# Four accumulators for the last feed-forward's gate-up tiles, one modulation row set moved between feed-forwards, and two later context loads

## The chip, the core and the metric

The program runs on one NeuronCore of a Trainium2 chip. The metric is the device time of one execution in microseconds (us). Engines are named as in the profile: PE (TensorE), DVE (VectorE), ACT (ScalarE), POOL (GpSimd), SP (SyncE, which here issues nearly all loads).

## What is computed

The input `x` (256 tokens, 1024 wide) goes through a first block of two hybrid layers and then through a second block of two layers, whose core is:

```python
for l in range(DEPTH):                       # DEPTH = 2
    mod_l = jax.nn.silu(c) @ ada_w[l] + ada_b[l]        # nine rows: shift, scale, gate, three times
    mod_c = jax.nn.silu(c_ctx) @ ada_w[l] + ada_b[l]
    sh1, sc1, g1, sh2, sc2, g2, sh3, sc3, g3 = ...split(mod_l, 9)
    csh1, ..., cg3 = ...split(mod_c, 9)
    xl = post_norm(xl, 0.5 * g1 * swiglu(modulate(xl, sh1, sc1), ffn1_w_in[l], ffn1_w_out[l]))
    xc = post_norm(xc, 0.5 * cg1 * swiglu(modulate(xc, csh1, csc1), ffn1_w_in[l], ffn1_w_out[l]))
    yc, yl = even_mixer(...) if l % 2 == 0 else odd_mixer(...)
    xl = post_norm(xl, g2 * yl)
    xl = post_norm(xl, 0.5 * g3 * swiglu(modulate(xl, sh3, sc3), ffn2_w_in[l], ffn2_w_out[l]))
    if not last:
        xc = ...the same with the context's rows
```

`swiglu(h)` is `(silu(gate) * up) @ w_out` with `gate, up = split(h @ w_in, 2)`, 1024 to 2 x 2816 and back. `xc` starts as the context `ctx` (256 x 1024).

## The kernel before, in words

Every weight matrix product is done in three passes, high times high, low times high, high times low (L445, L446, L447). A weight tile of 128 x 1024 is loaded by SP into a buffer `wr`, ACT makes the high part `wh` (L353) and DVE the low part `wl` (L440). Rows to be multiplied are transposed on PE (L538) into PSUM, modulated (L569 on DVE, or ACT), and split into `XTH` (ACT) and `XTL` (DVE, L571).

In order of time: first block layer 0 and layer 1 (`layer1`, 0 to 343 us), the first feed-forward of second-block layer 0 ("f1", to 695), the even mixer (to 977) with its output projection, the second feed-forward "f2" of layer 0 (to 1351), "f1" of layer 1 (to 1735), the odd mixer (to 1931) and the last feed-forward, "f2" of layer 1 for the latent rows alone. `ffn_two` runs the three feed-forwards with 512 columns (X and C together), `ffn_one` the last one with 256.

**Modulation rows.** Each pair `(l, c)` is one of the nine rows of layer l; c = 2, 5, 8 are gates. Those in `V1`, `V2`, `V3` are made by the generator `ada_v` inside the three `ffn_two` calls: for each, eight steps, each a 512 KB load (`in_adav`) and two DVE multiply-and-sum instructions into `vj` (L675, one for each of the two conditions). A gate then takes a bias (L681), a transpose on PE into a bank F (L683), a copy on ACT into `vr` and a write to memory by POOL (`g<-vr`, L686). `gate_rows` reads it back, spread over all partitions, as `gb` on SP's queue; the output passes multiply by `gb` in L590 and L808 before adding to the rows (L592, L594, L812). `fillv` lets the generator go a share of a step per gate-up tile and per output step: `VR` holds these shares for the three calls, and `VS` is the number of the gate-up tile in the first group from which it may begin. What is left is issued at the start of the last output passes by `fillv(1000)`.

**First block.** `layer1(0)` projects the rows in three parts, `rows_of(0)`, `rows_of(1)`, `rows_of(2)` (L445 to L447 into pA). Other modulation rows are made there by PE itself (`ada`: L635, a stationary `cs` times the weight tile, into pG), with weight tiles from a ring of two buffers (`RING[0]`). Between them stand the scores of the first block's index selection (L1136 on PE, ACT `rl`, L1144 and L1146 on DVE, closed by the mask in L1149), and the row transposes L1099. The context rows `C` are loaded by two SP loads behind `rows_of(0)` (L1104, `dma_late`: issued after the last load before it in the program). Their first user is the context's transposes in layer 0 of the first block.

**PSUM.** The last feed-forward has a pool of its own, `ps4`: four banks A for the output passes, two banks B, of which each holds gate and up of one tile of 256 columns, and two banks F for the transposes (`self.trt` names the tag that `tr_rows` takes).

The order of instructions on each engine is set by the scheduler of the framework from the program's order, the waits and the buffers, so a change of buffers or of a loop's share moves instructions around it too.

Of the kernel before, what the change touches and what calls it, by code (L numbers as in the profile page):

```python
# [20 lines left out]
P = 128  # L21
# [185 lines left out]
OB = "B"  # L207
HN = (1, 2)
TK = ((3, 2), (1, 4))
VS = 5  # L210
VI = (1, 1, 1)
F2 = (3, 3)
PUTV = (0, 1)
# [8 lines left out]
PS1 = {"A": 2, "B": 3, "F": 2, "G": 1}  # L222
BT = dict(tr="B", ada="G", trp="B", pc="B", dd="B", kc="B", idx="B", sc="B", sc2="B", cmp="B", pt="B", pcm="B", pool="B", wt="F", out="FA")

V1 = ((0, 3), (0, 4), (0, 5), (0, 6), (0, 7), (0, 8))
V2 = ((1, 0), (1, 1), (1, 2), (1, 3))
V3 = ((1, 4), (1, 5), (1, 6), (1, 7), (1, 8))
VR = ((2.4, 0.5), (1.75, 0.25), (2.2, 0.25))
FF1 = (0.5, 0.4)
FF2 = (0.7, 0.7)  # L230
EVF = 0.05
# [12 lines left out]
class Kern:  # L244
# [95 lines left out]
    def need(self, l, c):  # L340

        while (l, c) not in self.done:
            if (l, c) in V1 + V2 + V3:
                self.fillv(1)
# [580 lines left out]
    def ffn_two(self, name, l, pool, order, after, fills=(0, 0), vr=(0, 0), early={}):  # L925
# [8 lines left out]
        for f0 in range(0, NFT, G):  # L934
# [17 lines left out]
            for ft in range(f0 if f0 else F0, f1):  # L952
                self.ffn_in(wi, ft, hid[ft - f0], slice(0, 512), slice(0, 512), pool, "B")
                self.fill(fills[0])
                if f0 or ft >= VS:
                    self.fillv(vr[0])
# [83 lines left out]
    def layer1(self, l, b1):  # L1040
        nc, A, X = self.nc, self.A, self.X
# [30 lines left out]
        def rows_of(j):  # L1072
            n, R = XS1_N[j], (R0, R1, R2)[j]
            outs = self.xs(src, offs[j], n, 0, 2)
            for m in range(2):
                if j == 2:

                    for kv in range(2):
                        self.act(dds[kv][:, m].rearrange("p (r w) -> p r w", w=64),
                                 outs[m][:, None, 64 * kv:64 * kv + 64].to_broadcast([P, 2, 64]))  # L1080
                    self.act(R[:, m, 128:], outs[m][:, 128:n])
                else:
                    self.act(R[:, m, :], outs[m][:, :n])
# [15 lines left out]
                    nc.tensor.transpose(pt[:, jj * 256 + m * P:jj * 256 + (m + 1) * P], sr[m], self.ident)  # L1099
            return pt[:, :256], pt[:, 256:]  # L1100
        rows_of(0)
        if l == 0:
            for m in range(2):
                self.dma_late(self.C[m], A["ctx"][m * P:(m + 1) * P, :])  # L1104
        self.rope(R0[:, :, 0:288].rearrange("p m (h w) -> p m h w", w=32), r8c, r8s, 4, "rp")
        wi = self.small([P, 2, 8], "wi")
        nc.vector.tensor_scalar_mul(wi, R0[:, :, 480:488], 1.0 / 16.0)
# [43 lines left out]
        def topk(place):  # L1151
            if TK[l][0] <= place < TK[l][0] + TK[l][1]:
                i = place - TK[l][0]
                n = 8 // TK[l][1]
                for r in range(n):
                    for m in MO:
                        mx8 = self.small([P, 8], "mx8")
                        nc.vector.max(mx8, works[m])
                        nc.vector.match_replace(works[m], mx8, works[m], -3.3e38)
                if i == TK[l][1] - 1:  # L1160
                    for m in MO:
                        nc.vector.tensor_scalar(works[m], works[m], -3.2e38, NEG, op0=OP.is_gt, op1=OP.mult)
# [12 lines left out]
                self.stack_q(QS[:, 2 * (j + jj)], QS[:, 2 * (j + jj) + 1], pp[jj])  # L1175
        topk(1)
        rows_of(2)
        topk(2)

        pe = self.cols[:, C_PE + 16 * l:C_PE + 16 * l + 16]  # L1180
        pc = self.bank(BT["pc"])
        for kv in range(2):
# [6 lines left out]
            for par in range(2):  # L1189
                ps = slice(64 * par, 64 * par + 64)  # L1190
# [723 lines left out]
    def run(self):  # L1914
        tc, nc, A = self.tc, self.nc, self.A
# [3 lines left out]
        with tc.tile_pool(name="xc", bufs=1) as xc:  # L1919
# [6 lines left out]
            with tc.tile_pool(name="b1", bufs=1) as b1:  # L1926
                self.tp = b1
                with tc.tile_pool(name="ps1", bufs=2, space=PSUM) as ps:
                    self.ps, self.banks, self.trt, self.adat = ps, PS1, BT["tr"], BT["ada"]
                    self.gens, self.ring = [self.ada(0, (0, 1)), self.ctx_first(0, NC)] + [  # L1930
                        self.ada(l, [c for c in range(9) if (l, c) not in V1 + V2 + V3 + ((0, 0), (0, 1))]) for l in range(2)], (b1, "wa", RING[0])
                    self.layer1(0, b1)
# [14 lines left out]
            with tc.tile_pool(name="ff1", bufs=1) as ff:  # L1947
                self.accp = ff
                self.ring = (ff, "wa", RING[1])
                self.vgen, self.vlate = self.ada_v(V1, ff), VI[0]  # L1950
                self.ffn_two("f1", 0, ff, (1, 0), lambda w: self.xt_mod(0, 3, w) if stage > 4 else None, FF1, VR[0], dict(enumerate(self.hc)))
                self.settle()
# [9 lines left out]
        with tc.tile_pool(name="xd", bufs=1) as xc:  # L1962
            self.rows(xc)
            for i, t in enumerate(self.X + self.C):
                nc.gpsimd.dma_start(t, save[i])
            with tc.tile_pool(name="mo", bufs=1) as g:
                self.gbn, self.accp = 2, g
                self.mixer_out(A["evo"], 0, g, lambda i: self.defer(lambda: self.xt_mod(0, 6, 0), DF[3]) if i
                               else self.xt_mod(0, 6, 1))
            if stage == 5:  # L1970
                return self.store()
            self.gbn, self.phase = 2, 1
            with tc.tile_pool(name="ff2", bufs=1) as ff:
                self.accp, self.ring = ff, (ff, "wa", RING[2])
                self.vgen, self.vlate = self.ada_v(V2, ff), VI[1]
                self.ffn_two("f2", 0, ff, (1, 0), lambda w: self.xt_mod(1, 0, w) if stage > 6 else None, FF2, VR[1])
                if stage == 6:
                    return self.store()
                self.vgen, self.vlate = self.ada_v(V3, ff, self.cb), VI[2]
                self.ffn_two("f1", 1, ff, (1, 0), lambda w: self.xt_mod(1, 3, w) if stage > 7 else None, (0, 0), VR[2])  # L1980
            if stage == 7:
                return self.store()
            with tc.tile_pool(name="nm", bufs=1) as e:
                self.NH = self.tl(e, [P, KD, 256], "NH", dt=F32R)
                self.NL = self.tl(e, [P, KD, 256], "NL", dt=F32R)
                self.gbn, self.accp, self.phase = 1, e, 3
                with tc.tile_pool(name="na", bufs=1) as e2:
                    V = self.odd_values(e2, (1, 0))
                    ps2.__exit__(None, None, None)
                    ps3 = tc.tile_pool(name="ps3", bufs=2, space=PSUM)  # L1990
                    self.ps, self.banks = ps3.__enter__(), {"P": 2, "S": 3, "T": 2, "O": 1}
                    self.ptn = 5
                    self.odd(e2, V)
                gb = self.ogb
                outs = self.xs(A["nao"], 0, 512, 0, 2, xh=self.NH, xl=self.NL, tag="P")
                for m in range(2):
                    self.accum(self.X[m], 0, outs[m], gb, True)
                if TL[8]:
                    self.xs_tail(A["nao"], 4096, 0, self.X, gb, self.NH, self.NL, "S")
                else:  # L2000
                    outs = self.xs(A["nao"], 4096, 512, 0, 2, xh=self.NH, xl=self.NL, tag="P", rows=ROWS)
                    for m in range(2):
                        self.accum(self.X[m], 1, outs[m], gb, True)
                    self.layernorm(self.X)
                ps3.__exit__(None, None, None)
            if stage == 8:
                return self.store()
            with tc.tile_pool(name="ps4", bufs=2, space=PSUM) as ps:
                self.ps, self.banks = ps, {"A": 4, "B": 2, "F": 2}
                with tc.tile_pool(name="ff3", bufs=1) as ff:  # L2010
                    self.accp, self.phase = ff, 4
                    self.xt_mod(1, 6, 0)
                    self.holdl = [self.lastn] * 4
                    for _ in self.ffn_one("f2", 1, 0, ff, 8):
                        pass
# [65 lines left out]
```

## Time and profile before

| | us |
|---|---|
| median of 3 runs (lowest to highest) | 2138.78 (2134.31 to 2139.55) |
| the profiled execution's own time | 2137.89 |
| its span in the trace | 2136.1 |
| PE busy | 2080.0 (97% of the span) |
| DVE busy | 1544.2 (72%) |
| ACT busy | 840.3 (39%) |

The profiled execution lies 0.89 us under the median. The 1.8 us between its time and its span lie outside what the trace shows. PE is the engine with the work: it is idle for 56 us in all. So the places to look at are those where PE is idle or where its granted clock is at the lower of its two levels (2.4 and 1.2 GHz; 1.00 and 0.50 of full speed in the rows); a mean clock of 0.74 over 20 us is 10.4 us at the lower level. Elsewhere DVE, ACT and SP cost nothing unless PE waits for them.

### The profile page before, as it was taken

Reading aid. Unit: us, or ns where it says so; the run is one execution under the profiler, and the core shown is the slowest. Engines: PE = TensorE matmul, PEld = TensorE weight load, DVE = VectorE, ACT = ScalarE, POOL = GpSimd, SP = SyncE. Lnnn points to the kernel's source line nnn. Section 1 sums busy time; section 2 is a strip of 40 time slices with the busy share of each in tenths; the row PEclk is TensorE's granted clock in tenths of the full one; section 3 lists DMA queues with packets and bytes.
Section 4 is the critical chain, followed back from the end, with each engine's and each line's share of the span. In section 5 each row is a group of like instructions: output and inputs, shape, how many; then the busy total and the mean of one; then the engine's idle time right before and its main releaser. Section 6 shows DMA issues by size and latency. Waiting matters only on the chain.

```text
span 2136.1 us, 30784 instructions
## 1 busy us (share of the span) xinstructions
PE 2080.0 (97%) x11967; PEld 1761.8 (82%) x11967; DVE 1544.2 (72%) x2839; ACT 840.3 (39%) x1460; POOL 19.6 (1%) x43
## 2 busy tenths in 40 slices
PE   7999999999999999899999999999999999998998
PEld 5898888988888788788888888888888888888997
DVE  6877866668879785958467757857786876776666
ACT  5555544322221544545312222531322245654443
POOL 0000000000000000000000000000000000000000
PEclk9999999999999999999999999999999999998999
DMA  8546444746654311133645543355555435425663
GB/s 273 183 150 189 143 146 148 241 154 209 194 169 142 121 54 43 30 107 123 203 150 158 157 151 116 109 172 183 162 174 160 145 119 155 112 80 152 187 185 119
DMA packets 92627, 318.77 MB, mean 149 GB/s; under 512 B 10652, under 2 KB 15868, under 8 KB 92480
## 3 DMA queue, kind: packets, MB, share of 16 engines
q1 hardware_dynamic: 88736, 307.44, 46.9%
q0 software_dynamic: 2400, 5.72, 0.8%
q10 hardware_dynamic: 1344, 3.64, 0.5%
q8 instruction: 94, 1.54, 0.3%
q14 instruction: 53, 0.43, 0.1%
HBM read 313.93 MB, written 3.20 MB: 148 GB/s over the span
## 4 chain that ended last, share of the span: by engine, by line
PE 88%; DVE 7%; ACT 2%; issue 2%; DMA 1%; ACTq 0%; DVEq 0%; SPq 0%
PE pB L445 13%; PE pB L446 13%; PE pB L447 13%; PE pA L446 10%; PE pA L445 10%; PE pA L447 10%; PE pF L445 2%; PE pF L446 2%; PE pF L447 2%; PE pB L1551 1%; PE pP L445 1%; PE pP L446 1%; DVE wl L440 1%; PE pP L447 1%; PE pO L1909 1%
## 5 line engine op out<-in xcount | busy, mean ns | idle before, releaser
L353 ACT ACTIVATE wh<-wr 128x1024 fp32r<-128x1024 f32 (+4 forms) x424 | 442.5, 1046 | 980.0 <-issue 456.1
L440 DVE TENSOR_TENSOR wl<-wr,wh 128x1024 fp32r<-128x1024 f32 (+4 forms) x424 | 509.7, 1204 | 293.9 <-ACT wh L353 289.6
L445 PE MATMUL pB<-XTH,wh 128*128 128x512 f32 (+1 forms) x1552 | 537.4, 347 | 6.8 <-DVE hid L452 2.9
L446 PE MATMUL pB<-XTL,wh 128*128 128x512 f32 (+1 forms) x1552 | 536.2, 346 | 0.3
L447 PE MATMUL pB<-XTH,wl 128*128 128x512 f32 (+1 forms) x1552 | 535.1, 345 | 0.0
L445 PEld LDWEIGHTS pB<-XTH,wh 128*128 128x128 f32 x1552 | 294.0, 190 | 47.7 <-ACT XTH L353 3.8
L446 PEld LDWEIGHTS pB<-XTL,wh 128*128 128x128 f32 x1552 | 294.4, 190 | 38.7 <-DVE XTL L571 0.9
L447 PEld LDWEIGHTS pB<-XTH,wl 128*128 128x128 f32 x1552 | 294.6, 190 | 37.7
L675 DVE SCALAR_TENSOR_TENSOR vj<-wr,cb 128x1024 f32<-128x1024 f32 x240 | 293.1, 1221 | 4.0
L447 PE MATMUL pA<-wh,hid 128*128 128x512 f32 (+1 forms) x624 | 239.5, 384 | 0.0
L446 PE MATMUL pA<-wl,hid 128*128 128x512 f32 (+1 forms) x624 | 239.2, 383 | 0.0
L445 PE MATMUL pA<-wh,hid 128*128 128x512 f32 (+1 forms) x624 | 238.1, 382 | 0.0
L446 PEld LDWEIGHTS pA<-wl,hid 128*128 128x128 f32 x624 | 117.2, 188 | 24.3
L445 PEld LDWEIGHTS pA<-wh,hid 128*128 128x128 f32 x624 | 117.2, 188 | 23.6
L447 PEld LDWEIGHTS pA<-wh,hid 128*128 128x128 f32 x624 | 117.2, 188 | 23.2
L445 PE MATMUL pA<-wh,XTH 128*128 128x512 f32 (+4 forms) x336 | 126.1, 378 | 3.6 <-ACT wh L353 1.8
L446 PE MATMUL pA<-wl,XTH 128*128 128x512 f32 (+4 forms) x336 | 125.1, 373 | 1.6 <-DVE wl L440 1.4
L447 PE MATMUL pA<-wh,XTL 128*128 128x512 f32 (+4 forms) x336 | 125.2, 373 | 0.0
L758 DVE TENSOR_TENSOR pB<-ft,pB 128x512 f32<-128x512 f32 (+1 forms) x97 | 55.7, 574 | 95.1 <-PE pB L447 93.9
L590 DVE TENSOR_TENSOR pA<-pA,gb 128x512 f32<-128x512 f32 x74 | 51.5, 697 | 43.6 <-PE pA L447 37.6
L445 PEld LDWEIGHTS pA<-wh,XTH 128*128 128x128 f32 x336 | 65.1, 194 | 15.9 <-ACT wh L353 2.7
L446 PEld LDWEIGHTS pA<-wl,XTH 128*128 128x128 f32 x336 | 65.3, 194 | 12.8 <-DVE wl L440 3.1
(443 smaller groups left out, 2923.2 us busy)
## 6 DMA issues: line engine op xcount, KB each, us to landing
wr<-in_adav_dram SPq DMA_DIRECT2D x120, 512.0 KB, 4.5
wr<-in_f1i_dram SPq DMA_DIRECT2D x104, 512.0 KB, 3.6
wr<-in_f2i_dram SPq DMA_DIRECT2D x92, 512.0 KB, 3.9
wr<-in_f1o_dram SPq DMA_DIRECT2D x44, 512.0 KB, 3.7
wr<-in_f2o_dram SPq DMA_DIRECT2D x44, 512.0 KB, 3.7
wr<-in_w_dram SPq DMA_DIRECT2D x40, 512.0 KB, 4.2
wr<-in_na_dram SPq DMA_DIRECT2D x28, 512.0 KB, 4.1
wr<-in_ada_dram SPq DMA_DIRECT2D x24, 512.0 KB, 4.3
```

The source lines that it names most:

```text
L353: self.lasta = self.nc.scalar.activation(out, in_, func, **kw)
L440: i = eng.tensor_sub(lo[:, :w], raw[:, :w], h[:, :w].bitcast(F32))
L445: nc.tensor.matmul(out, lh, rh, start=start, stop=False)
L446: nc.tensor.matmul(out, lh, rl, start=False, stop=False)
L447: self.lastmm = nc.tensor.matmul(out, ll, rh, start=False, stop=stop)
L590: nc.vector.tensor_mul(p, p, gb[:, cs])
L675: nc.vector.scalar_tensor_tensor(junk, raw, 0.5 * f, cb[:, w], op0=OP.mult, op1=OP.mult, accum_out=gc[:, w, k:k + 1])
L758: nc.vector.tensor_mul(pgu[1], t, pgu[1])
L1551: nc.tensor.matmul(p[:, c0 + j * P:c0 + (j + 1) * P], K[r, j * 256 + tk * P:j * 256 + (tk + 1) * P], Q[r, j * 256 + tq * P:j * 256 + (tq + ...
L1909: nc.tensor.matmul(o[64 * hh:64 * hh + 64, m * P:(m + 1) * P], V[kt][:, h * 64:(h + 1) * 64], PTs[2 * hh + m][:, kt * P:(kt + 1) * P], sta ...
```

## The change

Three parts. The modulation row (0, 8), the gate of "f2" in layer 0, is made in the "f2" call itself instead of in the "f1" call before it; the share of `VR[1]` goes from 1.75 to 2.2 and all calls may begin one gate-up tile earlier. The two context loads go behind `rows_of(2)`. The last feed-forward's banks become four A and four B, and its transposes use the A banks.

```diff
-VS = 5
+VS = 4
...
-V1 = ((0, 3), (0, 4), (0, 5), (0, 6), (0, 7), (0, 8))
-V2 = ((1, 0), (1, 1), (1, 2), (1, 3))
+V1 = ((0, 3), (0, 4), (0, 5), (0, 6), (0, 7))
+V2 = ((0, 8), (1, 0), (1, 1), (1, 2), (1, 3))
 V3 = ((1, 4), (1, 5), (1, 6), (1, 7), (1, 8))
-VR = ((2.4, 0.5), (1.75, 0.25), (2.2, 0.25))
+VR = ((2.4, 0.5), (2.2, 0.25), (2.2, 0.25))
...
         rows_of(0)
-        if l == 0:
-            for m in range(2):
-                self.dma_late(self.C[m], A["ctx"][m * P:(m + 1) * P, :])
...
         topk(1)
         rows_of(2)
+        if l == 0:
+            for m in range(2):
+                self.dma_late(self.C[m], A["ctx"][m * P:(m + 1) * P, :])
         topk(2)
...
-                self.ps, self.banks = ps, {"A": 4, "B": 2, "F": 2}
+                self.ps, self.banks, self.trt = ps, {"A": 4, "B": 4}, "A"
```

SP in the first 20 us of `layer1(0)`. `w` tiles are the first block's weights, `ada` tiles those of PE's own modulation rows (ring of two). Before:

```order
L397 DMA wr_258<-in_w_dram 128x1000
L405 DMA C_3_97<-in_ctx_dram 128x1024
L405 DMA C_4_98<-in_ctx_dram 128x1024
L397 DMA wr_297<-in_w_dram 128x1024
L397 DMA wr_432<-in_ada_dram 128x1024
L397 DMA wr_442<-in_ada_dram 128x1024
L397 DMA wr_315<-in_w_dram 128x1024
```

After (tile names shift by two, 432 is now 430):

```order
L397 DMA wr_258<-in_w_dram 128x1000
L397 DMA wr_430<-in_ada_dram 128x1024
L397 DMA wr_295<-in_w_dram 128x1024
L397 DMA wr_440<-in_ada_dram 128x1024
L397 DMA wr_480<-in_ada_dram 128x1024
L397 DMA wr_490<-in_ada_dram 128x1024
L397 DMA wr_313<-in_w_dram 128x1024
```

The second pair of ada tiles (482 and 492 before, 480 and 490 now) moved up from behind all ten w tiles that follow 442; the context loads now stand behind the last of `rows_of(2)`'s w tiles, 601. On PE the products L635 with the first pair moved from behind `rows_of(1)` into the middle of `rows_of(0)`, and those with the second pair took their place there, ahead of the index scores instead of among them.

DVE at the end of "f1" in layer 0, from the last gate-up tile's split (`hid`) on. Before:

```order
L452 TENSOR_TENSOR hid_6065<-pB_6458,hid_6065 128x512
L675 SCALAR_TENSOR_TENSOR vj_4850,vg_6452<-wr_6525,cb_4847 128x1024 x2
L590 TENSOR_TENSOR pA_6577<-pA_6577,gb_4859 128x512
L675 SCALAR_TENSOR_TENSOR vj_4850,vg_6452<-wr_6529,cb_4847 128x1024
L594 TENSOR_TENSOR C_3_97<-C_3_97,pA_6577 128x512
L675 SCALAR_TENSOR_TENSOR vj_4850,vg_6452<-wr_6529,cb_4847 128x1024
L590 TENSOR_TENSOR pA_6598<-pA_6598,gb_4859 128x512
L675 SCALAR_TENSOR_TENSOR vj_4850,vg_6452<-wr_6533,cb_4847 128x1024
L594 TENSOR_TENSOR C_4_98<-C_4_98,pA_6598 128x512
```

After:

```order
L452 TENSOR_TENSOR hid_6065<-pB_6453,hid_6065 128x512
L590 TENSOR_TENSOR pA_6538<-pA_6538,gb_4859 128x512
L594 TENSOR_TENSOR C_3_97<-C_3_97,pA_6538 128x512
L799 BN_STATS lnst_6640<-C_3_97 128x6
L590 TENSOR_TENSOR pA_6559<-pA_6559,gb_4859 128x512
L594 TENSOR_TENSOR C_4_98<-C_4_98,pA_6559 128x512
L799 BN_STATS lnst_6680<-C_4_98 128x6
L590 TENSOR_TENSOR pA_6580<-pA_6580,gb_4861 128x512
L594 TENSOR_TENSOR X_1_95<-X_1_95,pA_6580 128x512
```

No L675 stands behind the last `hid` now; before, fourteen did, the last of them directly ahead of the first L808. The gate (0, 8) closes in "f2" of layer 0 instead, a few DVE rows ahead of the first L590 that needs it.

PE at the start of the last feed-forward (X's two row halves are transposed; the second half is normalised last). Before:

```order
L538 MATMUL pF_16940<-ident,X_1065_9024 128x128
L538 MATMUL pF_16951<-ident,X_1065_9024 128x128
L538 MATMUL pF_16940<-ident,X_1066_9025 128x128
```

After:

```order
L538 MATMUL pA_16940<-ident,X_1054_8985 128x128
L538 MATMUL pA_16951<-ident,X_1054_8985 128x128
L538 MATMUL pA_16962<-ident,X_1054_8985 128x128
L538 MATMUL pA_16973<-ident,X_1054_8985 128x128
L538 MATMUL pA_16940<-ident,X_1055_8986 128x128
```

Four transposes of the first half stand ahead of the second half's instead of two, and all sixteen ahead of the first gate-up product; before, eight of the sixteen stood among the products of the first two tiles.

## Rows read from the trace of the kernel before

**Rows 1.** The page's busy times: engine, busy us, share, instructions.
```profile
PE 2080.0 (97%) x11967; PEld 1761.8 (82%) x11967; DVE 1544.2 (72%) x2839; ACT 840.3 (39%) x1460; POOL 19.6 (1%) x43
```
**Rows 2.** By stretch: length, busy PE, PEld, DVE, ACT, POOL; PEclk, DMA share, GB/s.
```profile
375.00:400.00 25.00, 25.00 (x210) 24.93 (x209) 15.21 (x21) 11.67 (x18) 0.00 (x0) 1.00 0.72 212
```
**Rows 3.** The same view of `layer1(0)` and of the same steps in `layer1(1)`.
```profile
40.00:57.00 17.00, 13.47 (x116) 9.49 (x109) 8.67 (x26) 6.73 (x17) 0.00 (x0) 0.70 0.69 236
205.00:222.00 17.00, 16.68 (x110) 14.60 (x109) 13.41 (x40) 9.30 (x18) 0.00 (x0) 0.90 0.61 187
```
**Rows 4.** Timeline of SP: start, us, line, out<-in, count.
```profile
12.42 0.91 SPq L397 DMA_DIRECT2D wr<-in_ada_dram  x2
19.82 18.39 SPq L397 DMA_DIRECT2D wr<-in_w_dram  x10
40.52 1.02 SPq L397 DMA_DIRECT2D wr<-in_ada_dram  x2
```
**Rows 5.** Timeline of PE in `layer1(0)`; in brackets idle time before, and its releaser.
```profile
39.82 1.08 PE L635 MATMUL pG<-wr,cs 128*32 128x128 f32 x32
47.50 0.64 PE L635 MATMUL pG<-wr,cs 128*32 128x128 f32 x2 [3.52 <-DMA wr<-in_ada_dram]
```
**Rows 6.** Timeline of DVE: first and last step of the index scores, in both layers.
```profile
42.34 0.28 DVE L1144 TENSOR_SCALAR work<-rl,wi 128x128 f32<-128x128 f32 x1 [1.13 <-ACT rl L353]
...
58.28 0.29 DVE L1149 SCALAR_TENSOR_TENSOR work<-tab,work 128x128 f32<-128x128 f32 x1
...
211.84 0.28 DVE L1144 TENSOR_SCALAR work<-rl,wi 128x128 f32<-128x128 f32 x1
...
220.36 0.29 DVE L1149 SCALAR_TENSOR_TENSOR work<-tab,work 128x128 f32<-128x128 f32 x1
```
**Rows 7.** Tile C: the context's transposes, min/median/max ns, first and last start.
```profile
L538 PE MATMUL pB<-ident,C x16: 272/272/300, 130.3 to 134.6; 128*128 128x128 f32 x16
```
**Rows 8.** By stretch again: end of "f1" and of "f2", layer 0.
```profile
695.00:715.00 20.00, 15.58 (x98) 13.89 (x97) 17.14 (x62) 10.92 (x19) 2.79 (x6) 0.74 0.58 196
1351.00:1371.00 20.00, 18.62 (x128) 16.14 (x127) 19.02 (x54) 13.71 (x23) 0.00 (x0) 1.00 0.36 106
```
**Rows 9.** Timeline of DVE at the end of "f1" in layer 0.
```profile
664.91 1.22 DVE L675 SCALAR_TENSOR_TENSOR vj<-wr,cb 128x1024 f32<-128x1024 f32 x1
...
688.18 1.22 DVE L675 SCALAR_TENSOR_TENSOR vj<-wr,cb 128x1024 f32<-128x1024 f32 x1
...
698.29 0.54 DVE L824 TENSOR_SCALAR C<-C,lnmv,nwy 128x512 f32<-128x512 f32 x1
```
**Rows 10.** Timeline of PE behind "f1" and behind "f2", layer 0.
```profile
698.86 1.97 PE L538 MATMUL pF<-ident,C 128*128 128x128 f32 x8 [3.33 <-ACT C L353]
...
1358.31 0.39 PE L445 MATMUL pB<-XTH,wh 128*128 128x256 f32 x1 [1.06 <-ACT XTH L353]
```
**Rows 11.** Timeline of PE in the last feed-forward's first 25 us.
```profile
1929.13 1.54 PE L538 MATMUL pF<-ident,X 128*128 128x128 f32 x6 [2.63 <-DVE X L824]
...
1949.76 0.38 PE L445 MATMUL pB<-XTH,wh 128*128 128x256 f32 x1 [2.63 <-DVE hid L452]
```
**Rows 12.** By stretch: the 25 us behind that.
```profile
1950.00:1975.00 25.00, 25.00 (x197) 24.90 (x197) 12.75 (x19) 9.96 (x15) 0.00 (x0) 0.93 0.59 183
```
**Rows 13.** Timeline of DVE, first group's output passes of "f2", layer 0.
```profile
1084.48 1.22 DVE L675 SCALAR_TENSOR_TENSOR vj<-wr,cb 128x1024 f32<-128x1024 f32 x1
...
1092.85 0.69 DVE L590 TENSOR_TENSOR pA<-pA,gb 128x512 f32<-128x512 f32 x1
...
1100.92 0.69 DVE L590 TENSOR_TENSOR pA<-pA,gb 128x512 f32<-128x512 f32 x1
```
**Rows 14.** DMA issues: KB, median us to landing.
```profile
g<-vr POOLq DMA_DIRECT2D x5, 8.0 KB, 2.0
```
**Rows 15.** Tile g, gate rows: who waited (us, times); landing min/median/max.
```profile
  DVE pA L590: 5.9, 1
...
DMA to landing us min/median/max: 1.6/5.1/10.6
```

## The prediction, made before the changed kernel ran

> **What bounds the kernel now.** I read the busy times first: PE is busy for 2080.0 of 2136.1 us [rows 1], so 56 us of idle time and the time at the lower clock are all that a change in order or buffers can win. Then the table by stretch: inside the feed-forward loops PE is busy for 25.00 of 25 us at full clock [rows 2]; nothing is to be had there, and nothing is lost as long as DVE, ACT and the loads keep up. The chances lie at the seams. In `layer1(0)` PE idles 3.5 us of 17 and the mean clock is 0.70; the same steps in the second layer show 0.3 us and 0.90 [rows 3]. At the end of "f1" of layer 0 it idles 4.4 us of 20 at 0.74, while the end of "f2" shows 1.4 us at 1.00 [rows 8]. The last feed-forward's start has two stops of 2.63 us [rows 11]. Each of these three places is one part of the change. The timelines then say what ended each stop: a load of PE's own modulation tile [rows 5], the normalised context rows [rows 10], and the emptying of a gate-up bank [rows 11]. How I price the lower clock: a mean clock m over L us is 2 x (1 - m) x L us at half speed, and half of the busy part of that comes back if the clock stays up.
>
> **Part 1, the context loads in `layer1(0)`.** SP issues one pair of modulation tiles at 12.42, ten weight tiles from 19.82, and the second pair at 40.52 [rows 4], since the ring has two buffers and these come free only when PE has read the first pair at 39.82 [rows 5]. The second pair then meets PE's queue seven microseconds later: PE stands until 47.50, with the index scores behind it [rows 5], and DVE stands with it. In the new order both pairs are issued ahead of the ten weight tiles and PE reads the first pair inside `rows_of(0)`. The second pair is then there some 15 us before PE asks for it at about 40 us.
> What goes: idle time 3.53 - 0.32 = 3.2 us by the second layer's stretch [rows 3]. Half-speed time 2 x 0.30 x 17 = 10.2 us against 2 x 0.10 x 17 = 3.4 us; of the 6.8 us between, the busy share 13.47 / 17 = 0.79, halved, comes back: 2.7 us. Sum 5.9 us. A second look from DVE: the index scores take 58.28 - 42.34 = 15.9 us here and 220.36 - 211.84 = 8.5 us in the second layer [rows 6], so 7.4 us is the upper end.
> What it costs: sixteen L635 move into the first pass, half of the 1.08 us that thirty-two take [rows 5], and an equal number leaves the place behind `rows_of(1)`; net nothing, but if they stand there on a load that isn't in yet, that is new. SP now waits, ahead of the ten weight tiles, for PE to have read the first pair; before, it issued the first of these at 19.82 anyway [rows 4], and by its place in the order, between the products of the first two weight tiles, PE reads the pair at about that time (an estimate). Lower end: the idle time alone, less that 0.5 us: 2.7. The context rows come some 20 us later; their first reader is at 130.3 [rows 7], which hides it. I take **5.9 us** (2.7 to 7.4).
>
> **Part 2, one gate less in "f1" of layer 0.** Fourteen L675 stand on DVE from 664.91 to 688.18, behind the last gate-up tile, between the output passes' own steps [rows 9]. So the context's row sums start late, its normalised rows are there at 698.29 [rows 9], and PE, which is through with the output pass, waits 3.33 us for them and falls to the lower clock [rows 8, 10]. In the new order no L675 is left there: 40 steps instead of 48, and the shares of 2.4 and 0.5 give about 44 before the last group. Fourteen times 1.22 us [rows 9] leave DVE's path, 17 us, far more than PE's wait; what is late next is the usual seam, as behind "f2", where PE waits 1.06 us for the first `XTH` at full clock [rows 10].
> Gain by the two stretches: idle 4.42 - 1.38 = 3.0 us; half speed 2 x 0.26 x 20 = 10.4 us, times the busy share 0.78, halved: 4.1 us. **7.1 us**. Lower end 3.0, if the work in the half-speed stretch is paced by DVE (17.14 busy of 20, rows 8) rather than by PE; upper end 3.0 + 5.2 = 8.2.
>
> **Part 3, the gate in "f2" of layer 0.** Eight steps more, 16 L675 or some 20 us of DVE, spread over the loop: DVE is busy for 15.2 of 25 us where PE's loop is full [rows 2], so it is hidden; the next call has the share of 2.2 already. The gate is now made just before its use. By the order the last L675 of it stands where today one ends at about 1085.7 (1084.48 + 1.22); bias, transpose, ACT copy and POOL's issue I put at 1.5 us, an estimate, the write lands 2.0 us later [rows 14] and the read in 5.1, at worst 10.6 [rows 15]: `gb` is in at about 1094.5, at worst 1100. Its first reader, L590, runs at 1092.85 today [rows 13]; DVE waits 2 us. Behind it on DVE are the other three L590 and two `wl` tiles that PE wants 10 us later. PE itself needs the first bank again when the fourth tile of the pass is done, about 1100 by the fourth L590 at 1100.92 [rows 13], so there are some 4 us of cover. That such a wait can be free the trace shows: in "f1" L590 stood 5.9 us on its gate row [rows 15], in a stretch where PE was busy for 25.00 of 25 [rows 2]. **0**, bounds 0 and -2 us.
>
> **Part 4, banks of the last feed-forward.** The third gate-up tile waits 2.63 us for a bank that the first tile's `hid` releases [rows 11]; behind it the mean clock is 0.93 over 25 us, 3.5 us at half speed, all of it busy [rows 12], 1.75 us. With four banks the third tile needs none. Sum **4.4 us**. The other stop of 2.63 us, for the second half of X, stays [rows 11]. Sixteen transposes now stand ahead of the first product; before, eight stood among the products. That could cost up to 1 us, if the first products could have run sooner, since four of them take about 1 us at half speed (six took 1.54, rows 11). Ends: -1 and 4.4.
> Here one page speaks against the change. The trace shows a stop that ends with the release of a bank [rows 11]. The Trainium skill, "TensorE: Matmul & The Clock Gate", section "HAM oscillation — how this bites in real kernels", reports that in its kernel, once the loop kept the engine warm, a second set of PSUM buffers brought no further gain. By that, part 4 would be worth nothing; by the row it is worth 4.4 us. That is rival c below.
>
> **Sum.** 5.9 + 7.1 + 0 + 4.4 = 17.4 us. 2137.89 (the profiled execution's own time, 0.89 under the median) - 17.4 = **2120.5**.
>
> **Rivals.**
> (a) Part 1 gives nothing: SP stands on the first pair longer than I think, the ten weight tiles come late, and PE waits for them instead of for the modulation tile; or DVE's selection chain behind the scores is paced by something else. For it: the two w tiles and the pair share SP's queue [rows 4]. Against: the second layer, without this stop, ran the scores in 8.5 us [rows 6]. Time 2137.89 - 11.5 = 2126.4.
> (b) Part 2 gives its lower end, as the half-speed stretch is DVE's: 2120.5 + 4.1 = 2124.6. For it: 17.14 of 20 [rows 8]. Against: much of that DVE work is what the fourteen L675 had delayed.
> (c) The new banks give nothing, because the chain of transposes, `XTH` and `XTL` paces the first tiles, or a weight tile is late next: 2124.9.
> (d) Slower: the late gate. If `gb` lands after about 1100, PE stops in the loop of "f2", microsecond for microsecond, and a stretch of 10 us at half speed, as at the other stops, adds 5 us. It eats the gain of 17.4 only if `gb` is over 12 us later than 1100, and is slower than the kernel before by what lies beyond; with 20 us, 2120.5 + 25 = 2145.5. Against: the worst landing seen [rows 15] just fits.
> (e) The order that the scheduler makes opens new stops of the same size at these seams (the sixteen L635 in the first pass, the transposes' banks), and little is left: about 2135.
>
> **How the numbers follow.** Forecast 0.62, (a) 0.12, (b) 0.08, (c) 0.08, (d) 0.04, (e) 0.06. A measurement of this kernel tells about 0.3%, 6.4 us, from no change: below 2132.4 is faster. The forecast and (a) to (c) lie there, less 0.02 for two of these at once; so faster 0.88, same 0.08, slower 0.04. The range: with upper ends of parts 1 and 2 the sum is 20.0, or 2117.9; the three runs before spread by 2.6 us to either side, so 2115. At the other end two of the lower ends together (3.2 and 4.1, or 4.1 and 5.4) give 2128 to 2130, so 2131.
>
> **What would show it.** In the changed trace: no PE stop on a modulation tile near 44 us, a mean clock near 0.9 in that stretch, and index scores of 8 to 10 us. Behind "f1" of layer 0 no L675 among the L590, a PE stop near 1 us before the even mixer, clock 1.00. In "f2" PE busy for 25.00 of 25 through the first output passes, with L590 released by the gate's load after a wait of 2 us or so. In the last feed-forward no stop at the third gate-up tile. Wrong would be: SP's weight loads in `layer1(0)` shifted by several us and PE waiting on `wh`; a PE stop on the gate; a late first product in the last feed-forward as large as what the banks save.

## The result, and the profile of the changed kernel

| | before | changed |
|---|---|---|
| median, first occasion (4 runs each) | 2136.85 us | 2112.84 us (2112.43 to 2118.87) |
| ratio, with its 95% interval | | 0.990 (0.988 to 0.992) |
| the same kernel on a second occasion | 2137.1 | 2117.4, ratio 0.9911 (0.9894 to 0.9929) |
| on a third | 2136.23 | 2114.49, ratio 0.9907 (0.9888 to 0.9926) |
| span of the profiled execution | 2136.1 | 2111.0 |

The change makes the kernel 0.9% faster. The first median is 24.0 us under that of before and 2.2 us under the low end of the forecast's range; the median of all sixteen runs of the three occasions is 2115.2, some 21 us less, against a forecast of 2120.5.

Where the time went can be read by taking the same PE instruction (the n-th of its line and output) in both traces and subtracting its start times:

| place (us in the trace before) | changed minus before | step |
|---|---|---|
| 29, in `rows_of(0)` | +0.1 | |
| 129, end of `layer1(0)`'s selection | -7.6 | -7.7 |
| 684, last full products of "f1" | -7.9 | -0.3 |
| 712, first products of the even mixer | -13.8 | -5.9 |
| 772, in the even mixer | -18.4 | -4.6 |
| 1094, behind the gate in "f2" | -18.0 | +0.4 |
| 1919, end of the odd mixer | -17.6 | +0.4 |
| 1960, last feed-forward, first group | -23.4 | -5.8 |
| end of the span | -25.1 | -1.7 |

Three of the large steps lie where the change was made. The 4.6 us in the even mixer do not.

The page's busy line of the changed kernel (answers rows 1) and its stretches (length, busy PE, PEld, DVE, ACT, POOL, PEclk, DMA share, GB/s): the index scores (answers rows 3), the end of "f1" (answers rows 8, eight us earlier), the first output passes of "f2", and the last feed-forward's start.

```profile
PE 2061.5 (98%) x11967; PEld 1745.3 (83%) x11967; DVE 1545.5 (73%) x2839; ACT 839.0 (40%) x1460; POOL 19.5 (1%) x43
```
```profile
40.00:57.00 17.00, 16.29 (x140) 13.66 (x140) 14.93 (x45) 13.62 (x33) 0.00 (x0) 1.00 0.49 180
687.00:707.00 20.00, 17.87 (x137) 15.51 (x136) 16.76 (x49) 12.44 (x26) 2.07 (x5) 1.00 0.48 162
1057.00:1082.00 25.00, 24.95 (x110) 20.19 (x109) 19.84 (x32) 5.00 (x6) 0.50 (x1) 1.00 0.59 210
1908.00:1933.00 25.00, 21.96 (x154) 20.86 (x155) 19.97 (x39) 13.84 (x25) 0.00 (x0) 0.86 0.51 160
```

The first stretch has lost most of its idle time (3.5 us before, 0.7 now) and its lower clock (0.70, now 1.00). The second has lost half of its idle time (4.4 us before, 2.1 now) and its lower clock (0.74, now 1.00). In the third PE is idle for 0.05 us. In the fourth the lower clock is still there in part (0.86).

Over the whole span PE's idle time fell by only 6.6 of the 25.1 us (2136.1 - 2080.0 = 56.1 before, 2111.0 - 2061.5 = 49.5 now). The other 18.5 us are the same 11967 instructions of PE taking less time, most of it because fewer of them ran at the lower clock: the mean granted clock of the two profiled executions is 0.985 and 0.995, which by the forecast's formula is 64 and 21 us at half speed.

The timeline of SP in the changed kernel (start, us, out<-in, count; answers rows 4):

```profile
5.47 0.45 SPq L397 DMA_DIRECT2D wr<-in_ada_dram  x1
...
12.72 7.66 SPq L397 DMA_DIRECT2D wr<-in_ada_dram  x3
20.47 9.37 SPq L397 DMA_DIRECT2D wr<-in_w_dram  x6
29.89 0.90 SPq L405 DMA_DIRECT2D C<-in_ctx_dram  x2
```

All four modulation tiles are issued before the weight tiles at 20.47, which come 0.65 us later than the 19.82 of before. The timeline of PE shows the new short stop on the first pair, the pair's successor without a stop at 39.92 (answers rows 5), the first products behind "f1", the stop in the even mixer and the start of the last feed-forward (answers rows 10 and 11; in brackets idle time before and its releaser):

```profile
18.37 0.41 PE L635 MATMUL pG<-wr,cs 128*32 128x128 f32 x2 [0.67 <-DMA wr<-in_ada_dram]
...
39.92 1.08 PE L635 MATMUL pG<-wr,cs 128*32 128x128 f32 x32
...
691.07 0.30 PE L445 MATMUL pA<-XTH,wh 128*32 128x256 f32 x1 [0.68 <-ACT XTH L353]
...
742.45 1.68 PE L1551 MATMUL pB<-KQ 64*128 64x128 f32 x16 [2.15 <-issue]
...
1911.52 1.97 PE L538 MATMUL pA<-ident,X 128*128 128x128 f32 x12 [2.40 <-DVE X L824]
```

The timeline of DVE (lines of `layer1` are three less here): the index scores' first and last step (answers rows 6), the end of "f1" (answers rows 9), and the first L590 of "f2" (answers rows 13).

```profile
42.44 0.29 DVE L1141 TENSOR_SCALAR work<-rl,wi 128x128 f32<-128x128 f32 x1 [1.12 <-ACT rl L353]
...
52.19 0.29 DVE L1146 SCALAR_TENSOR_TENSOR work<-tab,work 128x128 f32<-128x128 f32 x1
...
656.39 0.68 DVE L452 TENSOR_TENSOR hid<-pB,hid 128x512 fp32r<-128x512 f32 x1
658.47 0.70 DVE L590 TENSOR_TENSOR pA<-pA,gb 128x512 f32<-128x512 f32 x1 [1.40 <-PE pA L447]
...
685.60 0.54 DVE L824 TENSOR_SCALAR C<-C,lnmv,nwy 128x512 f32<-128x512 f32 x1
...
1074.64 0.69 DVE L590 TENSOR_TENSOR pA<-pA,gb 128x512 f32<-128x512 f32 x1
```

The scores take 52.19 - 42.44 = 9.8 us instead of 15.9. At the end of "f1" DVE now waits for PE (1.40 us), and the context is normalised at 685.60 instead of 698.29, of which some 8 us are the shift from before that place. In "f2" L590 stands without a wait.

### The profile page after: what moved, and what is told of

Read it like the earlier page. It is cut to its first block, busy times and chain, and to the rows that moved or that the text cites. A ratio compares the mean times of both kernels' runs of the same rounds, so it can differ in the third digit from the quotient of the medians.

```text
span 2111.0 us, 30786 instructions
## 1 busy us (share of the span) xinstructions
PE 2061.5 (98%) x11967; PEld 1745.3 (83%) x11967; DVE 1545.5 (73%) x2839; ACT 839.0 (40%) x1460; POOL 19.5 (1%) x43
## 4 chain that ended last, share of the span: by engine, by line
PE 88%; DVE 6%; ACT 2%; DMA 2%; issue 2%; SPq 0%; ACTq 0%; DVEq 0%
PE pB L445 13%; PE pB L446 13%; PE pB L447 13%; PE pA L445 10%; PE pA L447 10%; PE pA L446 10%; PE pF L445 2%; PE pF L446 2%; PE pF L447 2%; DMA wr<-in_ada_dram 1%; PE pP L445 1%; PE pP L446 1%; PE pB L1551 1%; PE pP L447 1%; DVE wl L440 1%
## 5 line engine op out<-in xcount | busy, mean ns | idle before, releaser
L675 DVE SCALAR_TENSOR_TENSOR vj<-wr,cb 128x1024 f32<-128x1024 f32 x240 | 293.1, 1221 | 4.2
L445 PEld LDWEIGHTS pA<-wh,hid 128*128 128x128 f32 x624 | 117.3, 188 | 23.4
L590 DVE TENSOR_TENSOR pA<-pA,gb 128x512 f32<-128x512 f32 x74 | 51.4, 696 | 50.1 <-PE pA L447 44.0
```

Source lines behind the costliest of these rows:

```text
L445: nc.tensor.matmul(out, lh, rh, start=start, stop=False)
L590: nc.vector.tensor_mul(p, p, gb[:, cs])
L675: nc.vector.scalar_tensor_tensor(junk, raw, 0.5 * f, cb[:, w], op0=OP.mult, op1=OP.mult, accum_out=gc[:, w, k:k + 1])
```

## The experiments

The theory: each part acts at its own seam, by the stop that it removes and the half-speed stretch behind it, and the parts add up. The rivals are in each expectation. Steps of single traces below are differences of the same PE instruction against the trace of before, as in the table above. They tell where time went in one execution; what a kernel gains is told by its median against the median of before on the same occasion, and the two can be some us apart.

**Each part alone.** Only the context loads moved:

```diff
         rows_of(0)
-        if l == 0:
-            for m in range(2):
-                self.dma_late(self.C[m], A["ctx"][m * P:(m + 1) * P, :])
...
         rows_of(2)
+        if l == 0:
+            for m in range(2):
+                self.dma_late(self.C[m], A["ctx"][m * P:(m + 1) * P, :])
```

> The kernel before with the context loads moved behind rows_of(2) and nothing else. Theory (each part acts at its own seam): 7 to 8.5 us less than before, all of it in place by 130 us of the span; no PE stop on a modulation tile near 44 us, no half-clock stretch at 46 us; the seams at 695 and 1926 us as before. Rival (part 1 gives nothing alone, the gain needs the other parts): within 2 us of before. On the 10 us half-clock stretch behind the 2.1 us PE stop in the even mixer (present in the trace before, absent after, worth 4.5 us there): if it is a toss of the run, it may stand here or not; if part 1 removed it by shifting everything 8 us, it is absent here too.

2130.01 us, ratio 0.9974 (0.9962 to 0.9987). In the trace -8.1 us at 129, and the index scores' stretch is that of the changed kernel:

```profile
40.00:57.00 17.00, 16.30 (x139) 13.51 (x131) 14.89 (x44) 13.44 (x32) 0.00 (x0) 1.00 0.47 175
```

Part 1 stands on its own. A further 4.6 us went in the even mixer at 756, as in the changed kernel, although that seam was not touched. The profiled execution was the fastest of its eight; the median is 5.5 us under before.

Only the modulation row moved:

```diff
-VS = 5
+VS = 4
...
-V1 = ((0, 3), (0, 4), (0, 5), (0, 6), (0, 7), (0, 8))
-V2 = ((1, 0), (1, 1), (1, 2), (1, 3))
+V1 = ((0, 3), (0, 4), (0, 5), (0, 6), (0, 7))
+V2 = ((0, 8), (1, 0), (1, 1), (1, 2), (1, 3))
...
-VR = ((2.4, 0.5), (1.75, 0.25), (2.2, 0.25))
+VR = ((2.4, 0.5), (2.2, 0.25), (2.2, 0.25))
```

> The kernel before with the modulation row (0, 8) moved to the second feed-forward, its share 2.2 and the start one tile earlier, and nothing else. Theory: 5 to 7 us less than before, all at the end of the first feed-forward (no L675 behind the last gate-up tile, PE stop there under 1.2 us, no half-clock stretch there); nothing lost in the second feed-forward, to 0.5 us. Rival (the even mixer's 4.5 us come from this part, since the context's rows come earlier): 10 to 11 us less, and the half-clock stretch in the even mixer is absent here and present in the kernels without this part.

2131.68 us, ratio 0.9978 (0.9969 to 0.9988). The step at the end of "f1" is 5.8 us (from -2.0 at 670 to -7.9 at 730), 1.6 us more went in the even mixer, and in "f2" 0.4 us came back at the gate's transpose. The seam's stretch, 20 us:

```profile
693.00:713.00 20.00, 17.86 (x137) 15.47 (x136) 16.76 (x49) 12.59 (x26) 1.93 (x5) 1.00 0.50 162
```

Only the banks:

```diff
-                self.ps, self.banks = ps, {"A": 4, "B": 2, "F": 2}
+                self.ps, self.banks, self.trt = ps, {"A": 4, "B": 4}, "A"
```

> The kernel before with the last feed-forward's banks as four A and four B, transposes in A, and nothing else. Theory: 6 to 7.5 us less than before, 6 of them in the first group of gate-up tiles (54.8 us before, 48.7 after) and about 1 in the later groups (120.4 against 118.6 ns per product). Rival (from the notes, that more accumulator buffers bring nothing): within 1 us. The seams at 44 and 695 us as before.

2128.54 us, ratio 0.9971 (0.9957 to 0.9985). This run moves the transposes together with the banks, so it doesn't say yet whether more accumulators gain by themselves. The first group's 384 gate-up products take 48.0 us instead of 54.8, and the other seams are as before. The three medians together are 5.5 + 3.9 + 7.0 = 16.4 us under before; the whole change was 24.0, 19.7 and 21.7 us under it on its three occasions. Each of the three parts is known to 2 to 3 us, so the intervals allow the plain sum and don't exclude some us more.

**Which half of part 4.** First the transposes alone, with two gate-up banks:

```diff
-                self.ps, self.banks = ps, {"A": 4, "B": 2, "F": 2}
+                self.ps, self.banks, self.trt = ps, {"A": 4, "B": 2, "F": 2}, "A"
```

> The kernel before with the last feed-forward's transposes in the four A banks, but still two B banks for the gate-up tiles (two F banks lie idle). It tells what of part 4 is the transposes' and what the gate-up tiles'. Theory (two banks for gate-up stop the third tile): the stop of 2.6 us at the third tile stays or grows, since the first two tiles end sooner; 2 to 3.5 us less than before, from transposes that no longer stand among the products. Rival (all of part 4 is the transposes' place): 6 us less, no stop at the third tile.

Then four gate-up banks, with the transposes in two banks F as before. Two of the four banks A of the output passes go for it, so this is not the gate-up banks alone:

```diff
-                self.ps, self.banks = ps, {"A": 4, "B": 2, "F": 2}
+                self.ps, self.banks = ps, {"A": 2, "B": 4, "F": 2}
```

> The kernel before with four banks B for the last feed-forward's gate-up tiles, the transposes in two F banks as before, and two banks A (instead of four) for its output passes. Together with the kernel that only moved the transposes it tells which half of part 4 removes the stop of 2.6 us at the third gate-up tile. Theory from the last runs (the stop comes from the order, since transposes stand among the first two tiles' products and both end together; more gate-up banks remove it too, but the slow start stays): the stop is gone, 2.5 to 4.5 us less in the first gate-up group, 1 us less in the later ones, and up to 2 us given back in the output passes with two banks. Rival (the extra banks do nothing in the first group): the first group's gate-up products take 54 us as before.

2132.27 (ratio 0.9982, 0.997 to 0.9994) and 2132.64 us (0.9976, 0.9961 to 0.9991). The theory of the first run, that the stop would stay with two gate-up banks, was wrong: the stop at the third gate-up tile is gone in both traces, and the 384 products take 48.5 and 49.5 us; with both halves 48.0. With two banks A the last output passes cost 1.5 us, a stop of PE on L594. The first 25 us of that place in the kernel before, with the transposes in A, with four gate-up banks, and with both:

```profile
1925.00:1950.00 25.00, 18.20 (x114) 16.81 (x115) 19.16 (x38) 13.73 (x23) 0.00 (x0) 0.80 0.46 136
```
```profile
1925.00:1950.00 25.00, 20.81 (x153) 19.46 (x152) 20.02 (x41) 14.98 (x26) 0.00 (x0) 0.93 0.50 154
```
```profile
1925.00:1950.00 25.00, 20.44 (x142) 18.90 (x141) 19.39 (x39) 14.39 (x25) 0.00 (x0) 0.86 0.47 133
```
```profile
1925.00:1950.00 25.00, 20.82 (x153) 19.46 (x152) 20.18 (x42) 15.06 (x25) 0.00 (x0) 0.93 0.48 151
```

Each half alone wins back about the same part of PE's idle time (6.8 us before, 4.2 to 4.6 after). The mean clock is 0.93 and 0.86, but that ranks nothing: the changed kernel itself shows 6.8 us at the lower clock there in its first trace and 3.4 us in its second and third. So each half is a cure for the same stop, and which is the better one isn't shown. Nor is it shown that one half brings all of the time: by the medians the halves give 3.3 and 3.6 us and both together 7.0, with intervals of some 3 us to either side.

The timeline of DVE shows when the first and the second gate-up tile's bank are emptied, before and with the transposes in A alone:

```profile
1949.28 0.42 DVE L452 TENSOR_TENSOR hid<-pB,hid 128x256 fp32r<-128x256 f32 x1
1950.94 0.42 DVE L452 TENSOR_TENSOR hid<-pB,hid 128x256 fp32r<-128x256 f32 x1 [0.45 <-ACT hid L353]
```
```profile
1945.08 0.42 DVE L452 TENSOR_TENSOR hid<-pB,hid 128x256 fp32r<-128x256 f32 x1
1950.87 0.42 DVE L452 TENSOR_TENSOR hid<-pB,hid 128x256 fp32r<-128x256 f32 x1
```

With all sixteen transposes out first, the first tile runs through ahead of the second and its bank is empty 5.8 us before the second's; before, products of both tiles stood between the transposes, and both banks were emptied within 1.7 us. With four gate-up banks the first tile's bank is emptied as late as before (1949.29), and the third tile takes another.

**The stop in `layer1(0)`: the ring or the context.** A ring of three buffers, context loads where they were:

```diff
-RING = (2, 4, 4)
+RING = (3, 4, 4)
```

> The kernel before with a ring of three buffers instead of two for the modulation tiles of the first block (RING[0] = 3), context loads where they were. The first tile of the second pair can then be loaded before PE reads the first pair; only the second tile of it waits. Theory (the stop at 44 us comes from the ring's late load, and the context's place matters only because the scheduler fills the slot with a modulation tile): 3 to 7 us less than before, the stop on the modulation tile gone or under 1 us. Rival (the context's 1 MB itself delays the rest of the queue): no change within 1.5 us.

2133.66 us, ratio 0.9986 (0.9974 to 0.9998). The expectation that the stop would go was wrong: it moved. PE takes the first tile of the second pair at once now and stands on the second, whose buffer still comes free only behind the first pair:

```profile
42.07 0.64 PE L635 MATMUL pG<-wr,cs 128*32 128x128 f32 x14
...
48.28 0.63 PE L635 MATMUL pG<-wr,cs 128*32 128x128 f32 x2 [4.01 <-DMA wr<-in_ada_dram]
```

The stop goes with the tile that is loaded late, which is what the theory of the late load says; whether the context's megabyte in the queue matters beside that, this run doesn't tell. Its profiled execution was the slowest of its ten, 0.4 us behind before, so the 3.4 us of its median are not explained by that trace.

**Part 2 without the move.** Row (0, 8) stays in "f1", which is given a larger share:

```diff
-VR = ((2.4, 0.5), (1.75, 0.25), (2.2, 0.25))
+VR = ((2.8, 0.5), (1.75, 0.25), (2.2, 0.25))
```

> The kernel before with the share of the first feed-forward's call raised from 2.4 to 2.8 steps per gate-up tile, all 48 steps kept there. By the shares, 15 x 2.8 + 16 x 0.5 = 50, so none is left for the last output passes. Theory (only the fourteen L675 behind the last gate-up tile cost time): 5 to 6 us less than before at that seam, as with the row moved, and no loss in the loop. Rival (the first feed-forward has eight steps too many for its loads or DVE): PE stops inside the loop, less than 3 us gained.

2130.07 us, ratio 0.9975 (0.9962 to 0.9989), as with the move. The step at the seam is 4.8 us (+0.8 at 650 to -3.9 at 730), PE's idle time that of the other kernel, and 3.6 us of lower clock left:

```profile
694.00:714.00 20.00, 18.02 (x128) 15.83 (x126) 16.31 (x49) 12.29 (x24) 2.23 (x5) 0.91 0.50 167
```

Two of the fourteen L675 are left behind the last `hid` in this kernel. So it is the L675 behind the last gate-up tile that cost time, not the number of rows made in "f1". With parts 1 and 4 beside it, that is the changed kernel with `V1`, `V2` and `VS` as before and this share (the edit against the changed kernel):

```diff
-VS = 4
+VS = 5
...
-V1 = ((0, 3), (0, 4), (0, 5), (0, 6), (0, 7))
-V2 = ((0, 8), (1, 0), (1, 1), (1, 2), (1, 3))
+V1 = ((0, 3), (0, 4), (0, 5), (0, 6), (0, 7), (0, 8))
+V2 = ((1, 0), (1, 1), (1, 2), (1, 3))
...
-VR = ((2.4, 0.5), (2.2, 0.25), (2.2, 0.25))
+VR = ((2.8, 0.5), (1.75, 0.25), (2.2, 0.25))
```

> The changed kernel with part 2 and part 3 replaced: row (0, 8) stays in the first feed-forward, whose share goes from 2.4 to 2.8; VS, V2 and VR[1] as before. Theory (only the fourteen L675 at the seam cost time): as fast as the changed kernel to 1 us, perhaps 0.4 us faster, since nothing is made just in time in the second feed-forward. Rival (the move itself is worth more): 2 us or more slower than the changed kernel.

2118.38 us, ratio 0.9918 (0.9899 to 0.9937), against 0.9907 (0.9888 to 0.9926) of the changed kernel on the same chip: no difference that these runs can tell, and it is no better version.

**The gate made too late.** The forecast's slower case, made real by one exchange in the changed kernel:

```diff
-V2 = ((0, 8), (1, 0), (1, 1), (1, 2), (1, 3))
+V2 = ((1, 0), (0, 8), (1, 1), (1, 2), (1, 3))
```

> The changed kernel with (1, 0) and (0, 8) exchanged in V2, so that the gate row is made after eight more steps and what is missing of it is issued in one piece ahead of the output pass that needs it. It makes the wait for the gate as long as the forecast's slower case asked. Forecast's reckoning: the closing L681 comes some 15 to 20 us later on DVE, the gate's row is in 10 to 15 us after PE needs the first bank again, so PE stops 8 to 15 us and 0 to 5 us are added by a stretch at the lower clock: 8 to 20 us slower than the changed kernel, all in the first output passes of the second feed-forward. Rival (DVE's slack of the loop swallows it): within 2 us.

2141.72 us, ratio to before 1.003 (1.0014 to 1.0045): 24.3 us slower than the changed kernel on the same occasion, more than expected, and slower than before. In the trace 25.7 us come in at one place. PE's timeline there, and the 40 us of it:

```profile
1091.97 0.37 PE L683 MATMUL pF<-ident,vg 128*16 128x128 f32 x1 [10.49 <-DVE vg L681]
...
1104.31 0.76 PE L445 MATMUL pA<-wh,hid 128*128 128x512 f32 x1 [11.96 <-DVE C L592]
```
```profile
1075.00:1115.00 40.00, 17.54 (x66) 13.66 (x65) 26.18 (x43) 2.38 (x3) 0.50 (x1) 0.70 0.57 186
```

DVE's timeline of the same kernel shows the gate's last step and the wait for the row:

```profile
1091.65 0.17 DVE L681 SCALAR_TENSOR_TENSOR vg<-adabc,vg 128x16 f32<-128x16 f32 x1
...
1102.28 1.30 DVE L590 TENSOR_TENSOR pA<-pA,gb 128x512 f32<-128x512 f32 x2 [5.51 <-DMA gb<-g]
```

There are two stops, not one. The gate's own transpose (L683) stands in PE's queue among the output products, and none of those behind it runs while it waits 10.49 us for L681. Then the first bank is missing for 11.96 us. The mean clock of 0.70 over 40 us is 24 us at half speed. L681 came 24.2 us later than in the changed kernel (1067.45 there).

**The changed kernel again, twice, and with the larger ring.**

> The changed kernel itself, again, beside the kernel before on another occasion. The three parts alone gave 5.5, 3.9 and 7.0 us by their medians, 16.4 in all, while all together gave 24.0 (four runs each). Theory A (the parts add up, and the even mixer's half-clock stretch, worth 4.5 us, is present in most runs of the kernels with one part and absent in most runs of this one): 20 to 24 us less again, most runs within 1 us of 2112.5 and a few some 5 us higher. Theory B (the first four runs were lucky): 16 to 18 us less, runs spread evenly.

2117.4 us, ratio 0.9911 (0.9894 to 0.9929): between the two theories' numbers. What differs from the first trace of the same kernel is one place, the even mixer. Its stop of 2.1 us, marked "issue", is in every trace. The 15 us from just before or at it, in the kernel before, in the changed kernel's first trace and in its second:

```profile
755.00:770.00 15.00, 13.78 (x65) 11.31 (x66) 11.32 (x15) 3.99 (x4) 0.00 (x0) 0.66 0.14 39
```
```profile
741.00:756.00 15.00, 13.55 (x92) 11.10 (x92) 14.74 (x21) 5.61 (x7) 0.00 (x0) 1.00 0.18 50
```
```profile
741.00:756.00 15.00, 14.45 (x74) 11.95 (x75) 12.63 (x17) 3.32 (x4) 0.00 (x0) 0.77 0.18 49
```

The same program, the same stop, and the clock stays up in one execution and falls for 6.8 us (2 x 0.23 x 15 = 6.9) in the other.

> The changed kernel a third time, beside the two variants of it, so that these are compared on one chip. It gave 2112.84 in the first job and 2117.4 in the second. Expected 2112 to 2118, 18 to 24 us under the kernel before, with the runs spread over levels some 2 to 5 us apart, according to which stops are followed by the lower clock.

2114.49 us, ratio 0.9907 (0.9888 to 0.9926). Its trace has 1.00 in that stretch and a span of 2111.3.

The changed kernel with the larger ring:

```diff
-RING = (2, 4, 4)
+RING = (3, 4, 4)
```

> The changed kernel with a ring of three buffers for the modulation tiles. Theory (what is left there are stops of 0.7 and 0.5 us on modulation tiles): 0 to 1.5 us less than the changed kernel. Rival (an earlier modulation tile in SP's queue delays weight tiles): 0 to 2 us more.

2116.17 us, ratio 0.9908 (0.989 to 0.9926), the same as the changed kernel within the interval. None of the variants beats it.

## Why the prediction was right or wrong, step by step

**The sum.** Forecast 17.4 us, 2120.5; the three occasions gave 24.0, 19.7 and 21.7 us by their medians. Direction, size and places of three parts held. The range's low end of 2115.0 was too high for the first occasion, for two reasons: parts 1 and 4 were under-sized, and the even mixer was not thought of. That the sum came so near is luck in part: in the first trace parts 1 and 4 gave 3.2 us more than forecast, parts 2 and 3 1.6 us less, and 4.6 us came from a place that no part names.

**Part 1** (5.9 forecast; 7.7 in the trace, 8.1 alone). The mechanism was right: the late load, PE's stop, DVE's wait behind it. The term that was mis-sized is the clock. The idle time gave 2.8 us (3.5 to 0.7) against 3.2 forecast, so the clock gave some 4.9 against 2.7: I took the second layer's stretch, with 0.90, as what would be left, and the clock stayed at 1.00. The median of part 1 alone (5.5 us, to some 2.7 us) doesn't tell the forecast's 5.9 from the trace's 8.1. The stop on the first pair in `rows_of(0)`, which I allowed 0.5 us, is 0.67 us, in a place where PE idled before, and SP's weight tiles moved by 0.65 us, not by several: rival (a) did not come.

**Part 2** (7.1 forecast; 5.9 in the trace, 5.8 alone). Right in kind, 1.2 us too much. Both terms were a little too large: the idle time gave 2.3 us (4.42 before, 2.13 now) where 3.0 was assumed, and what is left of the step for the clock is 3.6 where 4.1 was assumed. The clock did go to 1.00, as forecast, so rival (b), which gives the clock's term to DVE's pace, did not come. That the backlog of L675 is the cause, the larger share without the move shows.

**Part 3** (0 forecast; 0.35 us in the trace). PE did not wait at the gate, and DVE did not either: `gb` was issued at 1070.24 and L590 ran at 1074.64 with no wait, where I had 2 us. It was close, since the two reads landed 3.9 and 4.8 us after their issue. The forecast left out the gate's own transpose, which now stands in PE's full loop:

```profile
1067.77 0.27 PE L683 MATMUL pF<-ident,vg 128*16 128x128 f32 x1
```

Nearly all of the 0.4 us that the table shows over "f2" comes in right at this place, 0.35 us. So do 0.35 to 0.42 us in the four other traces in which this gate is made in "f2" in time, and in the kernels that make it in "f1" nothing comes in at that place. Rival (d) is real, but its price was mis-sized: I had one stop and 5 us of clock, and left out the gate's transpose on PE's own in-order queue. With L681 24.2 us later the loss is 25.7 us, not the 17 that the stop for the bank (11.96) and 5 us would make.

**Part 4** (4.4 forecast; 5.8 in the trace, about 6.7 alone). Here the forecast's account of the cause was incomplete. "With four banks the third tile needs none" is true, as the kernel with four gate-up banks shows, but the bank is only one of two conditions of the stop. The transposes alone, with two gate-up banks, remove it too. What I had priced as a cost of up to 1 us, the sixteen transposes ahead of the first product, is a gain by itself. I had read the releaser's name (a bank, by `hid`) and not the order in front of it, which had put both tiles' ends within 1.7 us. The Trainium skill ("TensorE: Matmul & The Clock Gate", "HAM oscillation — how this bites in real kernels") reports of its kernel that PSUM double-buffering gave no further gain. Here four banks without the transposes' move bring 5.3 us at that place in the trace, since PE did stop on a bank. Once the transposes were moved, the two extra banks take the first group from 48.5 to 48.0 us, next to nothing; but the two medians, 2132.27 and 2128.54, lie further apart and their intervals overlap, so whether this kernel then agrees with the skill's isn't shown.

**Not forecast: 4.6 us in the even mixer.** In the traces of the five kernels that leave the earlier seams as they were (before, banks only, transposes only, gate-up banks only, ring of three) the stop of 2.1 us is followed by 10.2 us at the lower clock, in the last of them by 6.8. In the nine with part 1 or part 2 in some form the stretch is absent in five and 3.4 to 6.8 us long in four. So it goes with the earlier changes, but the same program shows it and doesn't show it, at the same stop. What decides it isn't settled: no run here changed that stop alone. Of the 4.2 us between the first and second trace of the changed kernel, 3.0 lie here (steps of 4.6 and 1.6 us). How much of the spread of the other runs it makes is not shown, since one execution of each is traced.

**Not a steady gain:** about 1.1 us of the last step in the table. The later gate-up products take 118.6 ns each in the first trace of the changed kernel and in that of the banks alone, and 120.0 in the six other traces with four gate-up banks, two of them of the changed kernel itself. With two gate-up banks they take 120.1 to 120.5.

## What to carry to other kernels

A stop is named after the last semaphore, and that names a cure, not the cause: before buying buffers, read in the order what stood ahead of the two things that ended at nearly the same moment. Price a stop with the half-speed stretch behind it, for here that was more than half of each gain, but keep a range for it, since the same stop has it in one run and not in the next. A step made just in time costs next to nothing while it is in time (0.35 us here); when it is late, count every in-order queue on which a piece of it stands, not only the one that waits for its result.

## What the runs showed of the hardware that was not expected

A PE stop of the same length in the same program (2.13 to 2.15 us) was followed by a mean clock of 1.00 over 15 us in two traces and of 0.77 in one; the cost of the lower clock there is a matter of the run. And the pace of products of 256 columns differs between two executions of one program by 1.2% (118.6 and 120.0 ns), with PE busy throughout and the clock at 1.00 in both.
